# Two LRU tiles in flight with 64-row gate products, pooling spread over filler and merge, 512-wide v and half of q/k, and another order of the filler

## The chip, the cores and the metric

One core of one Trainium2 chip runs the whole kernel in one launch. The metric is the device time of that launch in microseconds (us). Engines are named as the profile names them: PE (matmuls), PEld (the loading of a matmul's stationary operand), DVE, ACT, POOL, and SP, which issues most DMAs.

## The reference, cut to what matters

One encoder layer on 1024 tokens of width 1024. The input is normalised and multiplied by a 1024 x 9216 matrix; the columns are then split into branches of 512 columns and four merge gates of 1024:

```
z = rms_norm(x) @ w_in
a_x, a_g, q, k, v, b_g, c_x, c_g, d_x, d_g, merge = split(z)
y_a = rglru(a_x) * silu(a_g)                  # gated linear recurrence, both directions
y_b = neighbourhood_attention(q, k, v) * silu(b_g)
y_c = s5(c_x) * silu(c_g)                     # state space mixer, then a GLU
y_d = pool(d_x) * silu(d_g)                   # windowed means of 2, 4, 8, 16, then a 128x128 product
merged = sum_n (y_n @ w_branch[n]) * sigmoid(merge_n)
x = x + merged @ w_out
x = x + sigmoid(x @ ple_gate) * (p @ ple_proj)
```

In the recurrence (`rglru`) the convolved input `xc` passes two gates for each direction, `sigmoid(xb @ w + b)`, with eight 64 x 64 blocks in each weight, and then a scan `h[t] = a[t] h[t-1] + b[t]`.

## The kernel before, in words

Every large product is made in three passes to keep fp32 accuracy: each operand is split into a rounded part H (an ACT copy to fp32r) and a rest L (a DVE subtraction), and `mm3` (L87 to L94) issues H by H, H by L and L by H into the same PSUM bank. So a product over 1024 rows of contraction is 8 x 3 = 24 matmuls.

`z_gen` (L156) makes the product with `w_in` in units: one unit is 128 columns by 512 tokens, 24 matmuls 512 wide, into a PSUM bank of tag `z` (or alternately `z` and `t` when `zt` is "zt"). It is a Python generator, and its units are the filler, `fill`: most of the kernel's PE work is in it, 104 units, and they need nothing but the normalised input and their weights. A list in `run` (L1283) gives their order: the s5 input, the silu gates of branches (`branch_gate`, with a sigmoid on ACT and a product on DVE) and the merge gates (`gates`, a sigmoid on ACT alone).

The stages stand in this order: `start` (norm, the product p @ ple_proj, the first q/k), `attention`, `s5`, `glu`, `lru`, the rest of the filler, `pool` together with the loading of the first merge operand (`y_split`), `merge` (four branches in the order 1, 0, 2, 3) and `final`. In attention the loop itself takes filler: one step of the generator `side` after each of the 8 units of a round. The rounds 0 and 1 take the q/k product of round 2 and 3 (`at_z`, 8 steps of 24 matmuls, 256 wide); rounds 2 and 3 take one unit of `fill` each time. In `s5`, `glu` and `lru` a planner, `drive` (L187), adds up the PE and DVE microseconds that the stage and the filler declare in their `yield`, the stage's DVE figure multiplied by SC = (1.25, 1.35, 0.95), and emits filler as long as PE is behind. The order in which instructions are emitted is a priority only: the order in each engine's queue is fixed before the run by a list scheduler that works on modelled times, so that an instruction whose operands and buffers are there can come ahead of one that was emitted earlier.

`q`, `k` and `v` are made per token tile: `tok_gen` (L208) takes 128 tokens as the stationary operand and 256 columns of weights as the moving one. There are six such products of 8 tiles: four of q/k (one for each round, 128 columns of q and 128 of k) and two of v. `attention` runs v's two, then q/k of round 1, then the rounds.

An attention unit (`at_units`, L511) makes scores for two heads (4 matmuls into tag `s`), adds the bias and takes the maximum on DVE, exponentiates on ACT, normalises on DVE, transposes by 6 PE transposes into tag `t`, and copies them out on ACT; after every second unit `at_values` issues 24 matmuls of 128 x 64 with the values.

`lru` (L610) works on four tiles of 128 channels. A tile (`lru_tile`, L633) convolves on DVE, splits `xc`, and multiplies by four 128 x 128 gate matrices that hold two 64 x 64 blocks on the diagonal and zeros elsewhere (written by a POOL memset): 4 matrices x 2 halves x 3 passes = 24 matmuls, with a sigmoid on ACT after each half. The tanh, exp and square root on ACT, seven passes and two scans on DVE follow. All of its buffers are single, except for the input `up`.

`pool` (L695) generates its own 8 units of z and, at every second one, runs a `pool_tile` (L719): window sums by doubling adds on DVE, a split, 6 matmuls into tag `o`. `merge` (L1174) multiplies the branches; each result of 12 matmuls goes to `s` or `o` and is gated and summed on DVE.

## Time and profile before

| what | value |
|---|---|
| time, median of 3 runs (lowest to highest) | 1385.28 us (1384.99 to 1386.05) |
| the profiled execution's own time | 1385.52 us |
| its span, first to last instruction | 1383.7 us |
| matmuls in the span | 7450 |
| DMA | 181.99 MB, mean 132 GB/s |

A "start" in the views is counted from the first instruction of the span. A matmul's duration there is from its start to its modelled end, and a following one starts before that; the spacing of starts, not the duration, says how much of PE one takes. A granted clock of 1.00 is the higher of the two levels, 2.4 GHz.

### The profile page before, as it was taken

How to read it: one execution, taken by the hardware profiler on the slowest of the kernel's cores; microseconds unless marked ns; L12 is line 12 of the kernel's file. 1: busy time of each engine (PE TensorE's matmuls, PEld its weight loads, DVE VectorE, ACT ScalarE, POOL GpSimd, SP SyncE). 2: the span in 40 equal slices, each digit the busy share in tenths (PEclk: the TensorE clock that was granted, in tenths of full speed). 3: DMA queues.
4: the chain of work that ended last, by engine and by line, in shares of the span. 5: the costliest groups of instructions: out<-in, count | busy, mean ns of one | idle time of the engine just before them, and what ended most of it. 6: DMA issues, size and time to landing. Idle time of an engine off the chain costs nothing.

```text
span 1383.7 us, 19208 instructions
## 1 busy us (share of the span) xinstructions
PE 1368.5 (99%) x7450; PEld 1159.6 (84%) x7450; DVE 843.8 (61%) x1592; ACT 521.3 (38%) x825; POOL 20.6 (1%) x81
## 2 busy tenths in 40 slices
PE   7999999999999999999999999999999999999998
PEld 6999998888788888788888888888888888888886
DVE  6551766455299797979757556636566767732332
ACT  6542676588332222222243662644312212211211
POOL 2200000000000000000000000000000000000000
PEclk9999999999999999999999999999999999999999
DMA  9451223433443142324264143135527655333543
GB/s 323 130 146 59 72 77 118 133 105 109 100 127 99 61 129 89 114 88 127 91 213 142 35 140 110 61 137 188 213 94 258 206 175 176 135 108 128 179 144 119
DMA packets 141054, 181.99 MB, mean 132 GB/s; under 512 B 29200, under 2 KB 100888, under 8 KB 140962
## 3 DMA queue, kind: packets, MB, share of 16 engines
q1 hardware_dynamic: 140610, 180.72, 40.4%
q8 instruction: 59, 0.97, 0.3%
q14 instruction: 33, 0.27, 0.1%
q0 software_dynamic: 352, 0.03, 0.0%
HBM read 127.05 MB, written 54.03 MB: 131 GB/s over the span
## 4 chain that ended last, share of the span: by engine, by line
PE 93%; DVE 5%; DMA 1%; ACT 1%; issue 0%; SPq 0%; DVEq 0%
PE ps_z L92 19%; PE ps_z L93 19%; PE ps_z L94 19%; PE ps_t L97 4%; PE ps_t L93 4%; PE ps_t L92 4%; PE ps_t L94 4%; PE ps_o L92 3%; PE ps_o L93 3%; PE ps_o L94 3%; PE ps_s L92 3%; PE ps_s L93 3%; PE ps_s L94 3%; PE ps_o L578 2%; PE ps_s L543 2%; PE ps_s L1068 1%
## 5 line engine op out<-in xcount | busy, mean ns | idle before, releaser
L92 PE MATMUL ps_z<-hnH,wh 128*128 128x512 f32 x744 | 293.2, 394 | 2.0 <-DVE bgt L58 2.0
L93 PE MATMUL ps_z<-hnL,wh 128*128 128x512 f32 x744 | 292.0, 392 | 0.0
L94 PE MATMUL ps_z<-hnH,wl 128*128 128x512 f32 x744 | 291.9, 392 | 0.0
L64 DVE TENSOR_TENSOR wl<-wr,wh 128x1024 fp32r<-128x1024 f32 x88 | 107.4, 1221 | 110.4 <-ACT wh L80 109.6
L92 PEld LDWEIGHTS ps_z<-hnH,wh 128*128 128x128 f32 x744 | 139.8, 188 | 30.8 <-DVE bgt L58 2.4
L94 PEld LDWEIGHTS ps_z<-hnH,wl 128*128 128x128 f32 x744 | 139.8, 188 | 28.5 <-issue 0.4
L93 PEld LDWEIGHTS ps_z<-hnL,wh 128*128 128x128 f32 x744 | 139.8, 188 | 27.9 <-issue 0.4
L80 ACT ACTIVATE wh<-wr 128x1024 fp32r<-128x1024 f32 x88 | 93.0, 1059 | 166.3 <-PE ps_z L93 81.2
L92 PE MATMUL ps_z<-wh,hnH 128*128 128x256 f32 x384 | 108.3, 285 | 0.5 <-ACT zqk L80 0.5
L94 PE MATMUL ps_z<-wh,hnL 128*128 128x256 f32 x384 | 108.5, 287 | 0.0
L93 PE MATMUL ps_z<-wl,hnH 128*128 128x256 f32 x384 | 108.1, 283 | 0.0
L93 PE MATMUL ps_t<-hnL,wh 128*128 128x512 f32 x216 | 84.2, 390 | 0.0
L92 PE MATMUL ps_t<-hnH,wh 128*128 128x512 f32 x216 | 84.1, 389 | 0.0
L94 PE MATMUL ps_t<-hnH,wl 128*128 128x512 f32 x216 | 84.0, 389 | 0.0
L92 PEld LDWEIGHTS ps_z<-wh,hnH 128*128 128x128 f32 x384 | 73.2, 192 | 1.2 <-ACT zqk L80 1.2
L93 PEld LDWEIGHTS ps_z<-wl,hnH 128*128 128x128 f32 x384 | 73.5, 191 | 0.0
L94 PEld LDWEIGHTS ps_z<-wh,hnL 128*128 128x128 f32 x384 | 72.9, 192 | 0.0
L94 PE MATMUL ps_z<-wh,mL 128*128 128x512 f32 x128 | 51.0, 399 | 0.0
L549 DVE CUSTOM_DVE_ANT_0 sc<-ps_s,bias 128x384 f32<-128x384 f32 x64 | 34.2, 554 | 27.2 <-PE ps_s L543 14.6
L92 PE MATMUL ps_o<-myH,wh 128*128 128x512 f32 x128 | 49.9, 390 | 0.4 <-DVE pm L67 0.4
L92 PE MATMUL ps_z<-wh,mH 128*128 128x512 f32 x128 | 50.2, 393 | 0.0
L93 PE MATMUL ps_z<-wl,mH 128*128 128x512 f32 x128 | 50.0, 391 | 0.0
(371 smaller groups left out, 2596.9 us busy)
## 6 DMA issues: line engine op xcount, KB each, us to landing
wr<-in_w_in_dram SPq DMA_DIRECT2D x32, 1024.0 KB, 5.3
gd<-gz SPq DMA_DIRECT2D x32, 512.0 KB, 2.9
mgt<-gd SPq DMA_DIRECT2D x32, 512.0 KB, 4.2
sg<-bgt SPq DMA_DIRECT2D x16, 512.0 KB, 3.1
my<-yd SPq DMA_DIRECT2D x16, 512.0 KB, 4.2
mbr<-in_w_branch_dram SPq DMA_DIRECT2D x8, 1024.0 KB, 6.7
bias<-E SPq DMA_DIRECT2D x128, 48.0 KB, 2.0
xt<-in_x_dram SPq DMA_DIRECT2D x8, 512.0 KB, 10.0
```

Source lines behind the costliest of these rows:

```text
L64: self.nc.vector.tensor_tensor(out, a, b, ALU.subtract)
L80: return self.nc.scalar.activation(out, a, AF.Copy)
L92: mm(ps, aH, bH, start=(k == 0), stop=False)
L93: mm(ps, aH, bL, start=False, stop=False)
L94: mm(ps, aL, bH, start=False, stop=(k == n - 1))
L97: self.nc.tensor.transpose(ps, src, self.ident[:k, :k])
L543: nc.tensor.matmul(pss[h], q[h][:, qs], km[h][(slice(0, 128),) + ks], start=(p == 0), stop=(p == 1))
L549: nc.vector.tensor_tensor_reduce(sc, pss[h], bias[g][h][:, VIDX[j], :], 1.0, -3e38, ALU.add, ALU.max, mx)
L578: m = self.nc.tensor.matmul(po[64 * h:64 * h + 64, j * 128:j * 128 + 128], vb[:, g + c, j, h * 64:h * 64 + 64], PT[h][:, c * 128:c * 128 + ...
L1068: nc.tensor.matmul(py[:, c], Q[k][:, a, 1:9, :].rearrange("p t c -> p (t c)"), X[k][:, c], start=False, stop=(k == 1))
```

## The change

- v is made in one product 512 wide (8 tiles of 24 matmuls) instead of two 256 wide. The q/k products of rounds 2 and 3 are made as one product 512 wide too (`at_pair`), those of rounds 0 and 1 stay. Both take their split weights from three of the usual buffers (`whl`) and from the two buffers `gz`. The staging tile of v is 512 wide, and there is one of them instead of two.
- In attention, the q/k product of round 1 is no longer ahead of the rounds: two of its tiles stand beside each of the first four units of round 0. The pair's 8 tiles stand beside units 6 and 7 of round 0 and 0 to 5 of round 1. Units 6 and 7 of round 1 take one unit of filler each, and in rounds 2 and 3 every second unit does.
- SC becomes (1.5, 1.35, 0.8). The filler has another order, and the pooling input's 8 units are in it, ahead of the last merge gate. Three units (before: two) stand between s5 and glu, and their first matmul is placed behind the last s5 matmul on PE.
- In `lru_tile` the buffers of `xc`, the four gate outputs and `ls` are doubled. The gate weights are stored without zeros: 64 rows for each block, both directions beside each other. A gate product is 6 matmuls of 64 rows and 128 columns, 512 wide, alternating between rows 64 to 127 and rows 0 to 63 in a fixed order and into two banks (`s` and `o`). ACT then evacuates each of the four 64 x 512 quarters with its own bias; the biases come by two more small DMAs and two more PE transposes in `consts`.
- `pool` is cut in steps of its own and works from inputs that filler has already made. Its steps stand beside the rest of the filler (after the five steps of the first `y_split`) and then beside the merge's products. It uses `z` and `t` banks, and `whl` buffers for its weights.

```diff
-SC = (1.25, 1.35, 0.95)
+SC = (1.5, 1.35, 0.8)
...
+                if self.hold is not None:
+                    self.behind(first, self.hold)
                 yield 5.2, 0.55 + (f(ct, hf, ps) or 0.0)
...
+            br = tmp.tile([8, 2, 2, 64], F32, name="br")
+            for k, n in enumerate(("lru_b_r", "lru_b_i")):
+                nc.gpsimd.dma_start(br[:, k], i[n].rearrange("d (g c) -> g d c", c=64))
+                self.tr(pt[:, 80 + 8 * k:88 + 8 * k], br[:, k].rearrange("g d c -> g (d c)"), 8)
...
+        raw_v = self.wide_load("w_in", 2048)
...
-            self.tok_product(self.hnH, self.hnL, raw, put_v)
...
+        for t, ps in self.qkv_tiles(raw_v):
+            v = ap.tile([128, 512], F32, tag="vtok", name="vtok")
+            self.copy_a(v, ps)
+            nc.sync.dma_start(vd[t * 128:t * 128 + 128, :], v)
...
             for u, _ in enumerate(self.at_units(ap, rd, qk, bias, vd)):
-                next(side, None)
-                if u == 3:
+                if rd == 0 and u < 4:
+                    next(side)
+                    next(side)
+                elif rd < 2 or u % 2:
+                    next(side, None)
+                step = (rd, u)
+                if step == (0, 2):
+                    raw1 = self.qk_load(1)
+                if step in ((0, 3), (1, 5)):
+                    prep = self.at_prep(ap, rd + 1, zq[rd + 1])
+                    nxt = next(prep)
+                if step in ((0, 3), (0, 4), (1, 5), (1, 6), (2, 3)):
                     next(prep, None)
...
+                if step == (0, 5):
+                    side = self.at_pair(raw1)
+                    zq += next(side)
+                if step == (1, 5):
+                    side = fill
...
+    def qkv_tiles(self, raws):
+
+        hl = []
+        for q in range(4):
+            if q < 3:
+                H, L = self.whl([128, 2, 512])
+            else:
+                H, L = (self.gzp.tile([128, 2, 512], F32R, tag="gz", name="w" + c) for c in "hl")
+            self.split(H, L, raws[q // 2][:, q % 2 * 2:q % 2 * 2 + 2, :])
+            hl += [(H[:, k, :], L[:, k, :]) for k in range(2)]
+        for t in range(8):
+            ps = self.ps("z")
+            c = slice(t * 128, t * 128 + 128)
+            self.mm3(ps, [(self.hnH[k][:, c], self.hnL[k][:, c]) + hl[k] for k in range(8)])
+            yield t, ps
...
+        for m in range(2):
             for hf in range(2):
...
+                self.lru_gates(ct, m, slice(hf * 512, hf * 512 + 512), gH, gL, xH, xL, sg)
+                yield 0.9, 3.5
...
+        for k, (g, x) in enumerate(((gH, xH), (gH, xL), (gL, xH))):
+            for b in (1, 0):
+                r = rows[b]
+                i = self.nc.tensor.matmul(pss[b], g[r, m, :], x[r, c], start=(k == 0), stop=(k == 2))
+                if last is not None:
+                    self.behind(i, last)
+                last = i
+        for b, r in enumerate(rows):
+            for d, q in enumerate(rows):
+                self.act(sg[2 * m + d][r, c], pss[b][q], AF.Sigmoid,
+                         bias=self.gb[q, m, 2 * ct + b:2 * ct + b + 1])
...
+    def behind(self, later, earlier):
+
+        self.tc.add_manual_dep(later.ins, earlier.ins.name, mybir.DependencyInfo(
+            mybir.DependencyClass.NoSync, mybir.DependencyReason.DATA), reason="one run")
...
+            fill = self.z_gen([self.s5_u(), self.branch_gate(2, 3584), self.gates(1), self.gates(3),
+                               self.branch_gate(0, 512), self.gates(2), self.branch_gate(3, 4608),
+                               self.branch_gate(1, 2560), self.pool_part(), self.gates(0)])
...
-            next(fill)
-            next(fill)
             self.zt = "zt"
+            self.hold = self.last_y
+            for _ in range(3):
+                next(fill)
+            self.hold = None
             self.drive(self.glu(), fill, SC[1])
...
+                self.drive(self.lru(), fill, SC[2])
...
+                    side = itertools.chain(self.y_split(mp, mp, 1, Y), pool)
+                    for _ in fill:
                         next(side, None)
+                    while len(Y) < 4:
+                        next(side)
+                    self.merge(mp, mq, (1, 0, 2, 3), Y, side)
```

## Rows read from the trace of the kernel before

**Rows 1.** The page's part 1: busy time, share of the span, instructions.

```profile
PE 1368.5 (99%) x7450; PEld 1159.6 (84%) x7450; DVE 843.8 (61%) x1592; ACT 521.3 (38%) x825; POOL 20.6 (1%) x81
```

**Rows 2.** The page's part 4: the chain that ended last, by engine.

```profile
PE 93%; DVE 5%; DMA 1%; ACT 1%; issue 0%; SPq 0%; DVEq 0%
```

**Rows 3.** Windows by stage: length, then PE, PEld, DVE, ACT, POOL busy, clock, DMA.

```profile
262.00:366.00 104.00, 104.00 (x658) 87.02 (x656) 51.17 (x171) 78.05 (x139) 0.73 (x2) 1.00 0.35 107
407.00:703.00 296.00, 293.99 (x1702) 246.22 (x1701) 248.73 (x465) 65.56 (x104) 0.00 (x0) 1.00 0.33 102
750.00:952.00 202.00, 202.00 (x891) 166.94 (x890) 113.53 (x97) 103.14 (x125) 1.84 (x7) 1.00 0.29 101
1018.00:1200.00 182.00, 181.61 (x801) 150.01 (x800) 127.26 (x162) 41.47 (x41) 0.00 (x0) 1.00 0.53 178
```

**Rows 4.** Timeline of PE, q/k products 256 wide: start, duration, instruction.

```profile
152.52 0.28 PE L92 MATMUL ps_z<-wh,hnH 128*128 128x256 f32 x1
...
153.96 0.28 PE L92 MATMUL ps_z<-wh,hnH 128*128 128x256 f32 x1
```

**Rows 5.** Timeline of PE, filler units 512 wide.

```profile
860.14 0.39 PE L92 MATMUL ps_z<-hnH,wh 128*128 128x512 f32 x1
...
863.09 0.39 PE L93 MATMUL ps_z<-hnL,wh 128*128 128x512 f32 x1
```

**Rows 6.** Timeline of PE, LRU gate products between filler matmuls.

```profile
769.24 0.39 PE L93 MATMUL ps_s<-xL,gH 128*128 128x512 f32 x1
...
771.09 0.40 PE L93 MATMUL ps_z<-hnL,wh 128*128 128x512 f32 x1
```

**Rows 7.** Timeline of PE, s5's small-array products between filler (windows 426:432, 430.93:431.2).

```profile
429.47 0.39 PE L93 MATMUL ps_z<-hnL,wh 128*128 128x512 f32 x1
429.79 1.42 PE L973 MATMUL ps_s<-Q,Bb 64*32 64x128 f32 x60
...
430.69 0.52 PE L973 MATMUL ps_s<-Q,Bb 64*32 64x128 f32 x12
431.14 0.50 PE L94 MATMUL ps_z<-hnH,wl 128*128 128x512 f32 x1
431.48 0.39 PE L92 MATMUL ps_z<-hnH,wh 128*128 128x512 f32 x1
```

**Rows 8.** Groups of ACT by line and shape: count, busy us, mean ns, idle before.

```profile
L76 ACT ACTIVATE sg<-ps_o,vt 128x512 f32<-128x512 f32 x16 | 11.1, 695 | 0.0
L81 ACT ACTIVATE qd<-ps_t,gain 64x512 fp32r<-64x512 f32 x32 | 21.8, 683 | 7.3 <-PE ps_t L97 5.5 <-DVE ql L67 1.1
```

**Rows 9.** Timeline of PE in s5: a wait and what ended it.

```profile
556.35 0.50 PE L92 MATMUL ps_z<-hnH,wh 128*128 128x512 f32 x1 [1.65 <-DVE bgt L58]
```

**Rows 10.** Groups of PE from 158 to 366.7 us, the four rounds.

```profile
L92 PE MATMUL ps_z<-hnH,wh 128*128 128x512 f32 x157 | 61.9, 394 | 0.0
...
L92 PE MATMUL ps_z<-wh,hnH 128*128 128x256 f32 x80 | 22.8, 287 | 0.2 <-ACT zqk L80 0.2
```

**Rows 11.** The tiles yb and wh: durations min/median/max, first and last start.

```profile
L570 SPq DMA_DIRECT2D yd<-yb x4: 319/370/382, 200.4 to 366.7; - x4
L92 PE MATMUL ps_z<-hnH,wh x12: 387/390/397, 207.2 to 215.8; 128*128 128x512 f32 x12
```

**Rows 12.** Timeline of PE in round 0: the value products of successive unit pairs.

```profile
168.49 1.53 PE L578 MATMUL ps_o<-PT,vb 128*64 128x128 f32 x24
...
175.96 1.53 PE L578 MATMUL ps_o<-PT,vb 128*64 128x128 f32 x24
```

**Rows 13.** From the LRU to the merge: tile up, timeline of DVE, tile myL, timeline of PE.

```profile
L80 ACT ACTIVATE up<-ps_z x4: 598/598/599, 749.7 to 863.7; 128x512 f32<-128x512 f32 x4
...
950.84 1.22 DVE L58 TENSOR_TENSOR ls<-ls,sgl 128x1024 f32<-128x1024 f32 x1
...
L64 DVE TENSOR_TENSOR myL<-my,myH x4: 1225/1225/1226, 963.8 to 979.9; 128x1024 fp32r<-128x1024 f32 x4
...
1018.92 0.39 PE L92 MATMUL ps_s<-myH,wh 128*128 128x512 f32 x1
```

More of the change, by code (lines that the diff above doesn't have):

```diff
@@ L91, in mm3 @@
         for k, (aH, aL, bH, bL) in enumerate(pairs):
-            mm(ps, aH, bH, start=(k == 0), stop=False)
+            i = mm(ps, aH, bH, start=(k == 0), stop=False)
+            first = i if k == 0 else first
             mm(ps, aH, bL, start=False, stop=False)
             mm(ps, aL, bH, start=False, stop=(k == n - 1))
+        return first
     def tr(self, ps, src, k):
@@ L178, in z_gen @@
                 t = slice(hf * 512, hf * 512 + 512)
-                self.mm3(ps, [(H[:, k, :], L[:, k, :], self.hnH[k][:, t], self.hnL[k][:, t])
-                              for k in range(8)])
+                first = self.mm3(ps, [(H[:, k, :], L[:, k, :], self.hnH[k][:, t], self.hnL[k][:, t])
+                                      for k in range(8)])
+                if self.hold is not None:
+                    self.behind(first, self.hold)
                 yield 5.2, 0.55 + (f(ct, hf, ps) or 0.0)
@@ L216, in tok_gen @@
             yield 2.6, 0.0
-    def tok_product(self, aH, aL, raw, consume):
-        for _ in self.tok_gen(aH, aL, raw, consume):
-            pass
     def consts(self):
@@ L400, in attention @@
         vd = self.dp.tile([S, W], F32, name="vd")
-        z = [self.at_z(rd) if rd else self.z0 for rd in range(4)]
         zq = [self.zq0]
@@ L572, in at_values @@
     def at_values(self, po, vb, g, held, last):
-        before = last.ins
+        before = last
         for j, PT in held:
@@ L581, in at_values @@
                     if before is not None:
-                        self.tc.add_manual_dep(m.ins, before.name, mybir.DependencyInfo(
-                            mybir.DependencyClass.NoSync, mybir.DependencyReason.DATA), reason="one run")
+                        self.behind(m, before)
                     before = None
@@ L692, in lru_tile, with lru_gates, pool_u, pool_part @@
         nc.sync.dma_start(self.yd[0][ct * 128:ct * 128 + 128, :], s[0])
+    def lru_gates(self, ct, m, c, gH, gL, xH, xL, sg):
+        rows = [slice(64 * b, 64 * b + 64) for b in range(2)]
+        pss = [self.ps("so"[b]) for b in range(2)]
+        last = None
+        for k, (g, x) in enumerate(((gH, xH), (gH, xL), (gL, xH))):
[12 more added lines that the diff above has]
+            mybir.DependencyClass.NoSync, mybir.DependencyReason.DATA), reason="one run")
+    def pool_u(self, pu):
+        self.up = [pu.tile([128, 1040], F32, name=f"pup{k}") for k in range(4)]
+        for u in self.up:
+            self.nc.gpsimd.memset(u[:, 0:8], 0.0)
+            self.nc.gpsimd.memset(u[:, 1032:1040], 0.0)
+    def pool_part(self):
+        def put(ct, hf, ps):
+            self.copy_a(self.up[ct][:, 8 + hf * 512:8 + hf * 512 + 512], ps)
+        return 4096, 2, put
     def pool(self, pp):
-        nc, i = self.nc, self.i
+        nc = self.nc
         ef = pp.tile([128, 4, 16], F32, name="ef")
@@ L702, in pool @@
                 nc.gpsimd.memset(ef[:, g, 8 + t:9 + t], w / (w - t))
-        us = {}
-        def put_u(ct, hf, ps):
-            if hf == 0:
-                u = pp.tile([128, 1040], F32, tag="up", name="pup", bufs=2)
-                nc.gpsimd.memset(u[:, 0:8], 0.0)
-                nc.gpsimd.memset(u[:, 1032:1040], 0.0)
-                us[ct] = u
-            self.copy_a(us[ct][:, 8 + hf * 512:8 + hf * 512 + 512], ps)
-            if hf == 1:
-                self.pool_tile(pp, ct, us[ct], ef)
-            return 4.0
-        for c in self.z_gen([(4096, 2, put_u)]):
-            yield c
+        for g in range(4):
+            yield from self.pool_tile(pp, g, self.up[g], ef)
     def pool_tile(self, pp, g, u, ef):
@@ L1172, in branch_products, with merge @@
                     yield m, hf, gt, pb
-    def merge(self, mp, mq, order, Y):
+    def merge(self, mp, mq, order, Y, side):
         acc = [self.big.tile([128, 1024], F32, tag=f"bH{k}", name="acc") for k in range(8)]
@@ L1196, in merge @@
                     next(pre, None)
+                next(side, None)
             Y = nxt
@@ L1234, in final @@
             self.fw = itertools.count()
-            blocks = [(n, nb) for n in ("w_out", "ple_gate") for nb in range(2)]
+            blocks = [(n, 512 * nb) for n in ("w_out", "ple_gate") for nb in range(2)]
             raws = [self.wide_load(*blocks[0])]
-            for m, (n, nb) in enumerate(blocks):
+            for m in range(4):
+                nb = m % 2
                 if m < 2:
```

140 lines of the change are left out of this document (70 added, 70 removed).

## The prediction

> **What bounds the kernel now.** I read the page's busy line first: PE is busy for 1368.5 of 1383.7 us, DVE for 61% and ACT for 38% [rows 1]. A busy PE need not be at its peak, so the chain of waits comes next: PE holds 93% of the chain that ended last, DVE 5% [rows 2]. The windows by stage say the same from the rounds of attention to the end of the merge: PE is idle for 2.0 us in all of s5 and for 0.4 us in the merge, at a granted clock of 1.00, that is 2.4 GHz; DVE is nearest to a bound in s5, with 249 of 296 us [rows 3]. So there is next to no waiting to win back. The kernel gets faster only by what PE is spared, and slower by any new wait of PE. The spared time must be counted by the spacing of starts, since a matmul's duration covers the next start.
>
> **The change part by part.** The sum is made against the profiled execution, 1385.5 us, which is 0.2 us above the median of the runs; 1.8 us of it lie outside the span.
>
> *512-wide v and half of q/k.* Between 152.52 and 153.96 us lie 12 starts of 256-wide matmuls, 0.120 us each [rows 4]; between 860.14 and 863.09 lie 13 starts of 512-wide ones, 0.227 us each [rows 5]. Streaming 256 and 512 columns at 2.4 GHz takes 0.107 and 0.213 us, so each matmul pays about 0.013 us whatever its width, and 384 of 7450 matmuls go. Two old tiles take 48 x 0.120 = 5.76 us, a new one 24 x 0.227 = 5.45; v has 8 new tiles and the pair has 8: 16 x 0.31 = 5.0 us less. More cannot come of it, as no column is spared. Less can: a new tile wants all four splits of its weights, where the old one had two, so each of the two products could start a split late. The subtraction of such a split is 1.2 us by the same shape in rows 13; twice that leaves 2.6. I take 5.0: the last matmuls of the product before run meanwhile, and the fourth buffer pair (`gz`) is idle at that time. One staging tile for v instead of two is enough when a copy and its store end within a tile's 5.45 us; if SP is held by the value loads behind it, the second `z` bank covers one more tile.
>
> *Gate products of 64 rows.* The old ones: from 769.24 to 771.09 us lie eight starts, 0.231 us each [rows 6]; 96 of them are 22.2 us. The new ones are 96 too, in 16 runs of six, three for each half of the array's rows. If a half's matmul streams beside the other half's, a run is 3 x 0.227 = 0.68 us. What it costs to leave the full array and come back is read from s5's products of 64 rows and 32 columns. The step from a full matmul to the first small one is 0.32 us (429.47 to 429.79) instead of 0.227: +0.09. From 429.79 to 430.69, 48 small ones start 0.019 us apart; the last 12 need 0.23 at that rate, but the next full one starts 0.45 us after 430.69: +0.22. The full one after it is 0.34 us away: +0.11 [rows 7]. So a run costs 0.42 us beside its work. That makes 16 x (0.68 + 0.42) = 17.6 us, 4.6 us less than before. The bounds: if the switch were free, 10.9 us (11.3 less); if the halves did not stream side by side, 16 x (6 x 0.231 + 0.42) = 28.9 us (6.7 more). I take the value between, because the small products show both the switch and the overlap: a 128-column stream is 0.053 us at 2.4 GHz, and they start 0.019 apart [rows 7].
>
> The Trainium skill has a rule that speaks against this edit: changing the tiling mode drains the engine, while tiles of one mode work independently ("TensorEngine Tiling (Array Packing)", section Key Properties). Rows 7 agree with both halves of it; the page gives no price, and by the rule without one the term would lie anywhere from 11.3 less upward.
>
> The evacuation grows. A 64 x 512 activation takes as long as a 128 x 512 one, 0.683 against 0.695 us [rows 8], since ACT pays for columns. Before there were 32 such sigmoids, now 64: +22 us on ACT in the LRU, which had 103 of 202 us there [rows 3]. Each run then needs 4 x 0.69 = 2.8 us of ACT. It costs PE nothing while filler is there to run; without that cover it goes into the length of the LRU (second rival).
>
> *More filler in s5, less in attention and LRU.* The filler is moved, not removed, so PE's sum stays; what can change is waiting. Adding up the declared figures, `drive` gave s5 about 47 units and gives it 57 now. In the old list 24 of the 47 were silu units, whose product on DVE delays the release of their bank; such a product ended the wait of 1.65 us at 556 us [rows 9]. By the new list 14 of 57 are, and DVE's share falls. Of s5's 2.0 us of waits I take 1.0 as gone (bounds 0 and 2.0).
>
> *Attention with less filler.* Its loop now asks for filler in every second unit of rounds 2 and 3 and for none in units 4 and 5 of round 0. I cost this at 0, because the loop's place is only a priority. In the old rounds 157 first-pass matmuls of filler ran, 157 / 8 = 19.6 units where the loop asked for 16 [rows 10]. They began at 207.2 us, when only the first of four rounds had been stored (200.4), though the loop hands out filler from round 2 on [rows 11]. The scheduler pulls work ahead where PE would idle. The price without that cover is the third rival. ACT, 78 of 104 us in the later rounds [rows 3], gets relief, as fewer sigmoids stand between its exponentials.
>
> *Pooling beside filler and merge, three held units, consts.* The pool's 8 units of z and 24 matmuls stay. Its DVE work moves into a merge that has DVE at 127 of 182 us [rows 3], with the lightest part, the first branch, first: 0. The three held units give 16.4 us of PE work behind the last s5 product instead of 10.9 without the placing: 0. Two more small DMAs on POOL and two more transposes come well before PE reaches them: 0 (at most 0.2, two starts). The gate weights lose their POOL memset and keep their four DMAs a tile on SP.
>
> Sum: 1385.5 - 5.0 - 4.6 - 1.0 = 1374.9, so 1375 us. The term bounds by themselves give 1385.5 - 5.0 - 11.3 - 2.0 = 1367 and 1385.5 - 2.6 + 6.7 = 1389.6.
>
> **The rivals.**
>
> *The halves do not stream side by side.* For it: the only row products in the trace have 32 columns and four column groups, so their 0.019 us doesn't prove that two full-width halves overlap. Against it: 0.019 us is under half a stream. The gates then cost 6.7 us more, and the sum is 1385.5 - 5.0 + 6.7 - 1.0 = 1386.2: no change.
>
> *The LRU ends late, and PE runs dry ahead of the merge (the slower side).* The merge's first operand takes memory that the LRU holds. Before, the LRU lasted from 749.7 to 952.1 us, and the last split of that operand ended at 981.1, 29 us later; filler went on to 1018.9 [rows 13]. By the planner's figures 101 of the 112 units are handed out by the LRU's end, so LRU and tail together have 24 + 8 + 11 = 43 units, or 234 us with 5.45 us each, and 18 us of gates. If the scheduler runs 6 units ahead, as rows 10 suggest with its 3.6 in attention alone, 219 us are left. The LRU must then be done in 190. If it keeps its old 202 us, PE idles 12; if the 22 us of ACT lengthen it too, 34. I price it in the middle: 1375 + 23 = 1398. Against it: neither ACT (103) nor DVE (114) filled the 202 us [rows 3], so the single buffers and the amount of filler set that length, and two tiles in flight shorten it. The Trainium skill warns of the same place: tiling speeds up TensorE but not the evacuation of PSUM, which may become the bottleneck (same page, section PSUM Bottleneck); rows 8 agree with the cost for ACT.
>
> *Attention starves.* Of the 208.7 us of the old rounds filler took 3 x 157 x 0.23 and the 256-wide products 3 x 80 x 0.12, 137 us together [rows 10]; the 32 units' own matmuls are the rest, 2.2 us each. The fastest pace of units is two in 168.49 to 175.96, 3.74 us each [rows 12]. If the ten units without filler run at that pace with nothing beside them, PE idles 10 x 1.5 = 15 us: 1390. It decides as soon as the scheduler pulls nothing ahead; rows 11 are against it.
>
> *The switch is free.* Then 1367, as in the sum by bounds; rows 7 are against it.
>
> **How the numbers follow.** The forecast has 0.66, with a range of its own from 1369 to 1381; halves in sequence 0.10; late LRU 0.09; starving attention 0.09; free switch 0.06. The likeliest gives 1375. From 1366 to 1391 it takes in the free switch, the sequence and about all of the starving case, and leaves out most of the late LRU and the tails: a little over 8 in 10. What a measurement of this kernel tells from no change is about 0.2%, 2.8 us. Faster by more than that: the forecast, the free switch and a little of the slow cases made good elsewhere, 0.73. Within it: the sequence and small new waits, 0.12. Slower: 0.15.
>
> **What would show it.** The 256-wide matmuls fall to a third of their number, and 512-wide ones start 0.227 us apart in v. A gate run's six starts come in pairs, a few hundredths of a us between the two halves, about 0.23 us from pair to pair, and the first filler matmul starts late by some 0.2 us; if the six are 0.23 us apart each, the first rival holds. In s5 PE's idle time falls below 2 us. PE's idle time in the windows of attention and between the LRU's last product and the merge stays under 1 us; 10 us and more there would make the prediction wrong, with the LRU's last product or the scores as what ended the wait. The sigmoids of the gates are 64 of 64 x 512 at 0.69 us.

## The result, and the profile after

The changed kernel took 1408.95 us (median of 4 runs, 1407.08 to 1409.89) against 1385.13 us for the kernel before on the same chip: a ratio of 1.0169, 95% interval 1.0152 to 1.0187. Forecast were 1375 us, in a range from 1366 to 1391. In the profiled execution the span grew by 23.9 us, from 1383.7 to 1407.6.

The page of the changed kernel: TensorE's busy line, the granted clock in 40 slices, the chain that ended last.

```profile
PE 1376.7 (98%) x7068; PEld 1138.6 (81%) x7068; DVE 843.0 (60%) x1593; ACT 547.5 (39%) x851; POOL 19.9 (1%) x79
...
PEclk9999899999999999999999999999999999999999
...
PE 92%; ACT 4%; DVE 3%; DMA 1%; issue 1%; SPq 0%; ACTq 0%
```

PE has 382 matmuls fewer than in [rows 1], as it should, and yet is busy for 8.2 us more. The chain still belongs to PE, but ACT has 4% of it where [rows 2] had 1%. For a kernel whose PE is always busy I split PE's time by what it computes: for all matmuls of a kind, the time from start to next start, added up. So a wait counts with the kind that ran just before it, and a slow clock with the kinds that ran through it.

| us (matmuls) | before | after | c1_gates | f4_both |
|---|---|---|---|---|
| norm | 10.5 | 14.9 | 10.5 | 10.3 |
| input products, 256 wide | 141.5 (1152) | 50.1 (384) | 141.0 (1152) | 94.5 (768) |
| input products, 512 wide | 664.2 (2880) | 763.4 (3264) | 677.1 (2880) | 707.0 (3072) |
| attention | 73.8 | 79.0 | 73.7 | 73.9 |
| s5 | 48.8 | 55.3 | 48.8 | 46.4 |
| recurrence's gates (96) | 22.1 | 17.5 | 14.4 | 22.1 |
| merge (768) | 174.3 | 178.9 | 174.3 | 175.9 |
| all | 1376.1 | 1399.9 | 1382.1 | 1372.2 |

(The last two columns are experiments, below. The other kinds, 241 to 242 us in each column, are left out.) The gates fell by 4.6 us, and some 3 of their 17.5 us are waits among and behind the pairs: c1's pairs, which do not wait, take 14.4. All else that should fall or stay rose, the input products of both widths together from 805.7 to 813.5. The stretches where it happened, in windows of the changed kernel (length; PE, PEld, DVE, ACT, POOL busy; clock; DMA):

```profile
46.00:66.00 20.00, 17.53 (x123) 17.10 (x123) 8.36 (x13) 9.52 (x18) 0.73 (x2) 0.83 0.30 95
164.00:182.00 18.00, 13.30 (x44) 9.98 (x43) 9.43 (x21) 12.06 (x24) 0.00 (x0) 0.62 0.00 1
697.00:711.00 14.00, 8.17 (x34) 7.18 (x33) 6.96 (x11) 2.14 (x3) 0.00 (x0) 0.63 0.13 43
826.00:854.00 28.00, 24.82 (x110) 17.67 (x109) 16.47 (x17) 27.32 (x34) 0.00 (x0) 1.00 0.06 20
```

The kernel before has no such stretch in its norm, in round 0 or in its recurrence:

```profile
46.00:60.00 14.00, 14.00 (x122) 13.85 (x120) 7.02 (x15) 6.20 (x12) 1.98 (x4) 1.00 0.43 135
160.00:185.00 25.00, 24.53 (x218) 23.27 (x217) 19.84 (x70) 18.96 (x46) 0.00 (x0) 1.00 0.26 75
840.00:880.00 40.00, 40.00 (x178) 33.06 (x177) 15.79 (x14) 16.78 (x21) 0.00 (x0) 1.00 0.31 105
```

In the changed kernel's four PE idles 2.5, 4.7, 5.8 and 3.2 us, and in the first three the clock is low as well. At its two levels, a mean of 0.83 over 20 us is 6.8 us at 1.2 GHz, 0.62 over 18 is 13.7, and 0.63 over 14 is 10.4. The Trainium skill's table of the clock's states has these two levels, 1.2 GHz for an idle TensorE and 2.4 GHz for a busy one ("TensorE: Matmul & The Clock Gate", Part 1). The starts of 512-wide matmuls agree, 0.43 us apart in these stretches (175.35 to 175.78 below) and 0.227 elsewhere.

*46 to 66 us, the norm.* Timeline of ACT, then of PE; a bracket tells the idle time ahead of an instruction and what ended it:

```profile
46.67 1.06 ACT L82 ACTIVATE wh<-wr 128x1024 fp32r<-128x1024 f32 x1 [3.91 <-DMA wr<-in_w_in_dram]
47.63 1.25 ACT L83 ACTIVATE hnH<-ps_t,gT 128x512 fp32r<-128x512 f32 x2
```

```profile
48.35 0.58 PE L94 MATMUL ps_z<-wh,hnH 128*128 128x256 f32 x1 [3.77 <-ACT hnH L83]
48.73 0.41 PE L96 MATMUL ps_z<-wl,hnH 128*128 128x256 f32 x1
```

A split of v's wide weights stands in ACT's queue ahead of the norm's copies `hnH`, and waits for its DMA. Behind it wait the copies, and PE for them.

*164 to 182 us, round 0.* PE waits for the preparation of round 1 (`km`), for the copy `PT` that frees the transposes' bank, and then for `zqk`:

```profile
167.28 1.08 PE L101 MATMUL ps_t<-ident,zqk 128*128 128x128 f32 x4 [2.17 <-DVE km L69]
...
169.57 0.90 PE L101 MATMUL ps_t<-ident,sc 128*128 128x128 f32 x3 [0.58 <-ACT PT L82]
...
174.76 0.79 PE L94 MATMUL ps_z<-wh,hnH 128*128 128x512 f32 x1 [1.95 <-ACT zqk L82]
175.35 0.63 PE L96 MATMUL ps_z<-wl,hnH 128*128 128x512 f32 x1
175.78 0.63 PE L97 MATMUL ps_z<-wh,hnL 128*128 128x512 f32 x1
```

*697 to 711 us, the end of s5.* The three units are held behind the last s5 product, so in front of it PE has none:

```profile
701.76 0.80 PE L1139 MATMUL ps_s<-Xr,Q 128*128 128x128 f32 x2 [4.17 <-DVE Xr L66]
704.23 0.79 PE L1139 MATMUL ps_s<-Xi,Q 128*128 128x128 f32 x2 [1.67 <-DVE Xi L63]
```

*826 to 854 us, the recurrence.* ACT's queue there, and PE behind it:

```profile
842.45 1.38 ACT L78 ACTIVATE sg<-ps_o,gb 64x512 f32<-64x512 f32 x2
843.85 1.40 ACT L78 ACTIVATE sg<-ps_s,gb 64x512 f32<-64x512 f32 x2
845.27 1.06 ACT L82 ACTIVATE xH<-xc 128x1024 fp32r<-128x1024 f32 x1
846.24 1.04 ACT L82 ACTIVATE wh<-wr 128x1024 fp32r<-128x1024 f32 x1
```

```profile
846.38 0.49 PE L750 MATMUL ps_o<-xH,gH 64*128 64x512 f32 x1 [1.12 <-ACT xH L82]
847.33 0.50 PE L94 MATMUL ps_z<-hnH,wh 128*128 128x512 f32 x1 [0.46 <-ACT wh L82]
```

The gate pairs themselves, which answer to [rows 6, 7], do what the forecast said:

```profile
821.59 0.40 PE L97 MATMUL ps_z<-hnH,wl 128*128 128x512 f32 x1
821.92 0.50 PE L750 MATMUL ps_o<-xL,gH 64*128 64x512 f32 x1
821.92 0.50 PE L750 MATMUL ps_s<-xL,gH 64*128 64x512 f32 x1
822.26 0.39 PE L750 MATMUL ps_s<-xH,gL 64*128 64x512 f32 x1
822.26 0.39 PE L750 MATMUL ps_o<-xH,gL 64*128 64x512 f32 x1
822.48 0.39 PE L750 MATMUL ps_s<-xL,gH 64*128 64x512 f32 x1
```

Two halves start together. The step in takes 0.33 us, the first pair is followed by the second after 0.34, and later pairs are 0.22 apart.

### The profile page after: what moved, and what is told of

Same layout as the page of the kernel before. It is cut to its first block, busy times and chain, and to the rows that moved or that the text cites. A ratio compares the mean times of both kernels' runs of the same rounds, so it can differ in the third digit from the quotient of the medians.

```text
span 1407.6 us, 18440 instructions
## 1 busy us (share of the span) xinstructions
PE 1376.7 (98%) x7068; PEld 1138.6 (81%) x7068; DVE 843.0 (60%) x1593; ACT 547.5 (39%) x851; POOL 19.9 (1%) x79
## 4 chain that ended last, share of the span: by engine, by line
PE 92%; ACT 4%; DVE 3%; DMA 1%; issue 1%; SPq 0%; ACTq 0%
PE ps_z L94 19%; PE ps_z L97 19%; PE ps_z L96 19%; PE ps_t L101 4%; PE ps_t L94 3%; PE ps_t L96 3%; PE ps_t L97 3%; PE ps_s L97 2%; PE ps_o L97 2%; PE ps_s L94 2%; PE ps_o L96 2%; PE ps_s L96 2%; PE ps_o L94 2%; PE ps_o L632 2%; PE ps_s L597 1%; PE ps_s L1139 1%
## 5 line engine op out<-in xcount | busy, mean ns | idle before, releaser
L97 PE MATMUL ps_z<-hnH,wl 128*128 128x512 f32 x752 | 295.9, 393 | 1.1 <-DVE wl L66 1.1
L96 PEld LDWEIGHTS ps_z<-hnL,wh 128*128 128x128 f32 x752 | 141.5, 188 | 29.3 <-issue 1.3
L94 PE MATMUL ps_z<-wh,hnH 128*128 128x256 f32 (+1 forms) x256 | 88.6, 349 | 5.9 <-ACT hnH L83 3.8
L96 PE MATMUL ps_z<-wl,hnH 128*128 128x256 f32 (+1 forms) x256 | 88.4, 346 | 0.0
L97 PE MATMUL ps_z<-wh,hnL 128*128 128x256 f32 (+1 forms) x256 | 87.6, 347 | 0.1
L78 ACT ACTIVATE gz<-ps_z 128x512 f32<-128x512 f32 x54 | 31.9, 590 | 77.2 <-PE ps_z L97 41.8
L94 PEld LDWEIGHTS ps_z<-wh,hnH 128*128 128x128 f32 x256 | 50.1, 196 | 11.6 <-ACT hnH L83 4.0
L96 PEld LDWEIGHTS ps_z<-wl,hnH 128*128 128x128 f32 x256 | 50.1, 196 | 4.7
L97 PEld LDWEIGHTS ps_z<-wh,hnL 128*128 128x128 f32 x256 | 49.4, 195 | 5.4 <-DVE hnL L69 0.4
L97 PE MATMUL ps_s<-myH,wl 128*128 128x512 f32 x128 | 50.6, 395 | 0.2 <-DVE wl L66 0.2
L96 PE MATMUL ps_o<-myL,wh 128*128 128x512 f32 x128 | 50.5, 395 | 0.0
```

Of the source, the lines that this page charges most:

```text
L78: self.nc.scalar.activation(out, a, f, **kw)
L94: i = mm(ps, aH, bH, start=(k == 0), stop=False)
L96: mm(ps, aH, bL, start=False, stop=False)
L97: mm(ps, aL, bH, start=False, stop=(k == n - 1))
```

## The experiments

My theory after the traces (Theory A below): these are four separate losses, each set by what stands in one queue, and the merge's slower products (178.9 for 174.3 us) are a fifth. The rival (Theory B): the time goes in the long stages, and what is won early is given back.

### Three losses taken out of the changed kernel

**a1_nohold**

```diff
-            self.hold = self.last_y
             for _ in range(3):
                 next(fill)
-            self.hold = None
```

> The changed kernel, but the three units of filler behind s5 are not placed behind the last s5 product. Theory A (the loss is a handful of starts that TensorE waits for, each followed by a stretch at half clock): TensorE's two waits before the last s5 products (4.2 us on Xr, 1.7 us on Xi) and the half-clock stretch from 699.8 to 710 go, some 9 us: about 1400 us. Theory B (the time is lost in the long stages, the recurrence and the merge, and what is won earlier is given back there as a wait): 1407 to 1410 us, with the idle time coming back in front of the gated unit, where the held units had been TensorE's only work.

Measured: 1402.70 us, ratio to before 1.0121 (1.0103 to 1.0139). The waits between 690 and 720 us are gone, and 6.3 of 23.8 us come back, less than the 9 expected. In the profiled execution the clock fell at another place instead: between 836 and 848 us it is 0.72, behind waits of 1.1, 0.5 and 0.5 us in the recurrence like those that left it at 1.00 in the changed kernel. Its four executions go from 1398.5 to 1404.7 us.

**a2_norm**

```diff
-        for t, ps in self.qkv_tiles(raw_v):
+        for t, ps in self.qkv_tiles(raw_v, self.last_n):
...
-            self.split(H, L, raws[q // 2][:, q % 2 * 2:q % 2 * 2 + 2, :])
+            self.split(H, L, raws[q // 2][:, q % 2 * 2:q % 2 * 2 + 2, :], after)
```

(`last_n` is ACT's last copy of the norm.)

> The changed kernel, but ScalarE's copies of v's raw weights stand behind its last copy of the normalised input. Theory A: the 3.8 us wait on hnH at 48 us and the half-clock stretch behind it go, some 7 us: about 1402 us, with the last hnL copy back near 59 us. Theory B: v's weights are then late for its first tile, so that the wait moves to v's first product and the time stays within 2 us of 1409.

Measured: 1402.57 us, 1.0122 (1.0107 to 1.0137): 6.4 us back. The last `hnL` ends at 60.1 us instead of 66.8.

**a3_att**, and **a4_three**, which is a1, a2 and a3 together

```diff
         side = self.at_z(1)
         zq.append(next(side))
...
+        for _ in side:
+            pass
...
+            if rd == 0:
+                next(prep, None)
+                side = self.at_pair(raw1)
+                zq += next(side)
```

In both, the preparation of round 1 writes queries over those that round 0's first half still reads, so later units of round 0 compute with other queries than the reference's; the amount of work is the same.

> The changed kernel with the attention's work in another order: the q/k product of round 1 wholly ahead of the rounds, the whole preparation of round 1 at the start of round 0, the 512-wide product for rounds 2 and 3 beside all eight units of round 0, filler at every second unit of rounds 1 to 3. Theory A: the five waits of TensorE between 167 and 175 us (about 9 us together) and the half clock until 181 us go, the preparation of round 1 costs about 2 us of its own; some 8 to 10 us less: about 1400 us. Theory B: rounds 1 to 3 starve with filler in every second unit only, and the half clock appears there; within 3 us of 1409 or above.

> All three of the edits together. Theory A: the savings add, 9 + 7 + 9 us, because each stretch lies on TensorE's path and is given back nowhere: about 1384 us, the time of the kernel before. Theory B (given back later): less than half of the sum, above 1396 us.

Measured: a3 1414.53 us (1.0211), a4 1397.32 us (1.0082; 1.0065 to 1.0099). Theory A misses on a3, which is 5.6 us slower than the changed kernel, as Theory B had it, and on a4, which lies above B's 1396. a4 shows a reason: PE still waits 2.7 us on `km`, and between 120 and 160 us it is idle for 3.8 us. By the code the 512-wide product writes both `zqk` buffers, so it must follow round 1's preparation in any order, and the traces show nothing beside the preparation on PE. a4 gives back 11.6 us in all; a1 and a2 by themselves give 12.6. So either the two add and the order wins nothing, or they add a little less; a1 with a2 alone was not run.

### Parts of the change, put into the kernel before

**c1_gates**: the 64-row gates (`lru_gates`, the bias table) as in the change. **c2_widev**: v in one 512-wide product, split behind the norm. **c3_both**.

```diff
-                self.mm3(ps, [(gH[:, m, :], gL[:, m, :], xH[:, c], xL[:, c])])
-                self.act(o[:, c], ps, AF.Sigmoid, bias=v[:, 5 + m:6 + m])
...
+                self.lru_gates(ct, m, slice(hf * 512, hf * 512 + 512), gH, gL, xH, xL, sg)
```

```diff
-            self.tok_product(self.hnH, self.hnL, raw, put_v)
...
+        for t, ps in self.qkv_tiles(raw_v, self.last_n):
```

> The kernel before with one part of the change: the recurrence's gates as pairs of 64-row products (and their bias table), its buffers, its order and all else as before. Theory A (the gates are worth what the prediction said, the loss lies elsewhere): gates 44.5 us of TensorE in the first kernel against 39.4 in the changed one, both with their waits; 4 to 5 us less than before, about 1381 us. Theory B (the 64 evacuations of half a tile hold ScalarE, which splits the next weights and recurrence tiles, and TensorE waits 4 to 5 us as it does at 846 to 852 us in the changed kernel): same as before within 1 us or slower.

> The kernel before with one part of the change: v as one 512-wide product, with its weights' splits behind the norm's last copy so that they hold nothing up. Theory A: 384 products of 256 columns at 0.123 us become 192 of 512 columns at 0.227 us, 47.2 against 43.6: 3 to 4 us less, about 1382 us. Theory B (the wide tiles wait for weights or for a buffer): no gain.

> The kernel before with both of these parts. Theory A: they add, 7 to 8 us less than before, about 1377.5 us: faster than both kernels. Theory B (one gives back what the other wins, in the slack ahead of the merge): 1381 us or above.

Measured: c1 1391.54 us, 1.0045 (1.0032 to 1.0058). c2 1384.33 us, 0.9991 (0.9983 to 1.0000). c3 1389.37 us, 1.0028 (1.0018 to 1.0039). Theory B holds for c1 and c3; c2's 1.1 us lie between its two theories, at the edge of what the runs tell apart. The pairs are a surprise. (The 44.5 and 39.4 us expected for gates include some 22 us of the GLU's own.) They take 7.7 us off the gates (table), more than in the changed kernel, and make the kernel 6.1 us slower. c1's PE, between the recurrence and the merge:

```profile
1001.04 1.22 PE L92 MATMUL ps_o<-pmH,pwH 128*128 128x512 f32 x2 [5.48 <-ACT pmH L80]
1002.05 0.63 PE L92 MATMUL ps_z<-hnH,wh 128*128 128x512 f32 x1
```

The recurrence's last gate product ends 9.7 us later (944.3 for 934.6), the pooling behind it comes late, and PE waits 5.5 us and goes on at 1.2 GHz. Two shorter waits, of 1.1 us for `wh` at 794 and of 1.7 us for `wl` at 855, come before. v wide wins 1.1 us; on PE 141.5 - 95.4 less and 708.4 - 664.2 more, 1.9 us.

**g1_evac64** tells whether it is the pairs or their evacuation:

```diff
-                self.act(o[:, c], ps, AF.Sigmoid, bias=v[:, 5 + m:6 + m])
+                for q in (slice(0, 64), slice(64, 128)):
+                    self.act(o[q, c], ps[q], AF.Sigmoid, bias=v[q, 5 + m:6 + m])
```

> The kernel before with nothing changed but the evacuations of the recurrence's gates: each 128-row sigmoid is cut into two of 64 rows, 64 in all; TensorE's products stay as they were. Theory A (what the pairs lose is ScalarE's time: 64 evacuations at 0.68 us instead of 32 at 0.69, 21.6 us more): TensorE's gates stay near 22.1 us, and yet the kernel is 8 to 14 us slower, the 6 us that the pairs lost in the kernel before plus the 8 that they won on TensorE: about 1397 us, with the wait in front of the pooling's products near 1000 us that the pairs had (5.5 us). Theory B (the loss comes from the pairs themselves, from their switches or their tables): within 1.5 us of before.

Measured: 1398.42 us, 1.0093 (1.0075 to 1.0111): 12.7 us slower with not one product changed (gates 22.1 us). Theory A, though the wait is in another place than forecast. g1's ACT, then PE:

```profile
791.98 1.28 ACT L76 ACT_TABLE_LOAD   x1
793.28 1.38 ACT L76 ACTIVATE sg<-ps_s,vt 64x512 f32<-64x512 f32 x2
794.68 0.63 ACT L80 ACTIVATE gH<-gw 128x512 fp32r<-128x512 f32 x1
795.34 1.38 ACT L76 ACTIVATE sg<-ps_o,vt 64x512 f32<-64x512 f32 x2
796.74 1.06 ACT L80 ACTIVATE wh<-wr 128x1024 fp32r<-128x1024 f32 x1
```

```profile
797.85 0.80 PE L92 MATMUL ps_z<-hnH,wh 128*128 128x512 f32 x1 [4.84 <-ACT wh L80]
798.44 0.63 PE L93 MATMUL ps_z<-hnL,wh 128*128 128x512 f32 x1
```

The filler's next weights `wh` stand behind the sigmoids; a second wait, of 3.1 us for `wl`, comes at 853. Halves of an evacuation cost 0.684 us each, as [rows 8] say; and between 700 and 1060 us ACT loads its tables 21 times instead of 14 (18 in c1), 1.28 us each. The prediction's second rival was right that the evacuations would tell. It was wrong on where PE would feel them: in the middle of the recurrence, with filler at hand, and not ahead of the merge. The Trainium skill says that tiling speeds up TensorE but not the evacuation of PSUM, and that the copy may become the bottleneck after a fourfold speedup ("TensorEngine Tiling (Array Packing)", section PSUM Bottleneck). Here the doubled evacuations cost 12.7 us with PE's products unchanged.

### The changed kernel repaired, and its gates and attention exchanged

**e3_place** is a1 and a2 together and

```diff
-                with tc.tile_pool(name="po", bufs=1, reuse_waits="tile") as pp, \
-                        tc.tile_pool(name="mp", bufs=1, reuse_waits="tile") as mp, \
-                        tc.tile_pool(name="mq", bufs=1, reuse_waits="tile") as mq:
+                with tc.tile_pool(name="mp", bufs=1, reuse_waits="tile") as mp, \
+                        tc.tile_pool(name="mq", bufs=1, reuse_waits="tile") as mq, \
+                        tc.tile_pool(name="po", bufs=1, reuse_waits="tile") as pp:
...
-        self.up = [pu.tile([128, 1040], F32, name=f"pup{k}") for k in range(4)]
+        self.up = [pu.tile([128, 1088], F32, name=f"pup{k}")[:, 0:1040] for k in range(4)]
```

> The changed kernel without the held units and with the norm's order mended, and then the merge's two pools put ahead of the pooling's in memory, so that the merge's operands lie lower (from 134208 bytes of a partition instead of 146624) and at the same offset in 2 KB as the rest. The first two edits alone should give 1396 us (6.3 and 6.4 us less, if they add). Theory A (where the operands lie sets the merge's pace of 0.232 us for each product instead of 0.227): the pace falls to 0.227, 768 x 0.005 = 4 us less: about 1392 us. Theory B (the pace comes from the pooling beside it, or from elsewhere): 0.232 stays, 1396 us.

Measured: 1390.54 us, 1.0034 (1.0022 to 1.0045); the merge's products are back at 0.227 us. If a1 and a2 add, that is 5.8 us for the place; the products alone are 3.7 us faster (178.9 to 175.2). e3's six executions go from 1387.3 to 1392.7 us, and the profiled one is near the lowest.

**f1_gates128**: e3 with the gates of the kernel before. **f2_att256**: e3 with its attention, v wide. **f4_both**. **f5_onedeep**: e3 without the `bufs=2` of `xc`, `sg`, `ls`.

```diff
-                self.lru_gates(ct, m, slice(hf * 512, hf * 512 + 512), gH, gL, xH, xL, sg)
...
+                self.mm3(ps, [(gH[:, m, :], gL[:, m, :], xH[:, c], xL[:, c])])
```

```diff
-                    side = self.at_pair(raw1)
...
+                side = z[rd + 2]
```

> The changed kernel with its three repairs (no held units, the norm's order, the merge's place; 1390.5 us), and in it the gates of the kernel before: 96 products on all rows instead of the pairs, 32 evacuations of 128 rows instead of 64 of 64 rows; recurrence two tiles deep as in the changed kernel. Theory A (the pairs win nothing once ScalarE's 22 us more of evacuation hold up the splits): TensorE's gates 22.1 instead of 17.0 us, but its waits on ScalarE's and VectorE's splits between 804 and 833 us (5 us) go: same within 1.5 us. Theory B (with the pooling beside the merge the evacuations are hidden and the pairs win their 5 to 8 us): 4 us or more slower, 1395 us or above.

> The same repaired kernel (1390.5 us) with the attention of the kernel before, but v 512 wide: the q/k products of rounds 1 to 3 in 256 columns, round 1's whole ahead of the rounds, those of rounds 2 and 3 beside rounds 0 and 1, filler at every unit of rounds 2 and 3. Theory A (round 0 loses some 9 us to waits and the half clock behind them, because the preparation of round 1 and the product for rounds 2 and 3 must follow one another within it): 384 more products of 256 columns cost 1.5 us, the 9 us go: about 1383 us. Theory B (filler that the attention takes is missed later, in s5 or the recurrence): 1388 us or above.

> Both: the repaired kernel with the gates and the attention of the kernel before. What is left of the change is v 512 wide, the recurrence two tiles deep, and the pooling beside filler and merge. Theory A: about 1382 us, the gates neutral, the attention's 7 us won; faster than both kernels by some 3 us. Theory B (the pairs win): 1387 us or above.

> The repaired kernel (1390.5 us) with the recurrence's buffers one tile deep as before, its gates in pairs. Theory A (two tiles deep keeps the tail of the recurrence off TensorE's path): it comes out 2 us or more slower, with waits of TensorE on the recurrence's splits above 5 us in all. Theory B (the depth buys nothing, since there is filler to run beside it): within 1.5 us.

Measured, before at 1386.14: f1 1391.51 us (1.0037), f2 1397.30 (1.0081; 1.0067 to 1.0094), f4 1381.38 (0.9966; 0.9954 to 0.9979), f5 1393.81 (1.0059). So f4, with the old gates and the old attention, beats both kernels. Theory A holds for f1, f4 and f5, Theory B for f2. Gates and attention cannot be priced apart. With old gates the old attention is worth 10.1 us (f1 to f4), and in f4 PE waits nowhere between 150 and 180 us; with the pairs the old attention costs 6.8 (e3 to f2). With the new attention the pairs are worth 1 us at most (f1 to e3), with the old one they cost 15.9 (f4 to f2). Two tiles deep is worth some 3 us (f5 to e3; the intervals touch), and PE's waits in the recurrence are 5.6 us without it, 3.2 with it. f2's PE from 1000 to 1060 us, where the merge begins:

```profile
PE ps_s L96 <- ACT myH L82: 4.8, 2, 3.2
PE ps_s L96 <- ACT wh L82: 2.4, 1, 2.4
PE ps_s L98 <- DVE myL L66: 2.1, 1, 2.1
PE ps_o L96 <- DVE acc L60: 1.7, 1, 1.7
```

(waited for: us, times, longest). The old attention uses more filler, less is left beside the recurrence, and the merge's first operand `myH`, late by the pairs' evacuations, comes bare. With the old gates (f4) the same attention has one wait there, of 1.3 us.

**g2_lessfill** (f2) and **g4_lessfill128** (f4) test that:

```diff
-                next(side, None)
+                if rd < 2 or u % 2:
+                    next(side, None)
```

> The repaired kernel with the old attention (1397.3 us), with filler at every second unit only in rounds 2 and 3, so that 8 units more (43 us of TensorE's work) are left for s5 and the recurrence. Theory A (the pairs lost 16 us there because the filler ran out beside the recurrence, and ScalarE's and VectorE's late work was left bare at the merge's start, 1010 to 1053 us): the waits at the merge's start go, the attention loses 2 to 4 us: about 1385 us. Theory B (the merge's late start has another cause): 1395 us or above.

> The kernel with the repairs, the old attention and the old gates (1381.4 us), with filler at every second unit only in rounds 2 and 3. Theory A (with whole-row gates ScalarE has the room, filler was not short, and the only wait of 1.5 us at the merge's start is all there is to win): the attention loses 2 to 4 us and the merge wins 1.5: 1382 to 1384 us. Theory B (filler is short here too): below 1380 us.

Measured: g2 1385.56 us, 1.0000 (0.9990 to 1.0009), 11.7 less than f2, with 1.4 us of waits left at the merge's start: theory A. g4 1389.39 us, 1.0028 (1.0018 to 1.0039), 8.0 more than f4: neither theory. Its ACT and PE:

```profile
811.32 1.28 ACT L78 ACT_TABLE_LOAD   x1
812.62 0.69 ACT L78 ACTIVATE sg<-ps_o,vt 128x512 f32<-128x512 f32 x1
813.20 0.68 ACT L78 ACTIVATE sg<-ps_s,vt 128x512 f32<-128x512 f32 x1
813.77 1.06 ACT L82 ACTIVATE wh<-wr 128x1024 fp32r<-128x1024 f32 x1
```

```profile
814.88 0.50 PE L96 MATMUL ps_z<-hnH,wh 128*128 128x512 f32 x1 [2.16 <-ACT wh L82]
...
817.41 0.79 PE L96 MATMUL ps_s<-xH,gH 128*128 128x512 f32 x1 [1.80 <-ACT xH L82]
```

With filler shifted by eight units, a weight split meets a run of table loads and sigmoids that it misses in f4. So the amount of filler is only a part of it; where it falls on ACT's queue is another. And with this filler the pairs win: g2 is 3.8 us faster than g4, where f2 is 15.9 slower than f4.

### What slows the merge's products

Three versions of f4 that differ in where the merge's operands lie in a partition (what is allocated next to them moves too). In f4 they begin at 134208 bytes, 64 past a multiple of 512; in the changed kernel at 146624, 192 past.

```diff
-pu.tile([128, 1088], F32, name=f"pup{k}")[:, 0:1040]
+pu.tile([128, 1040], F32, name=f"pup{k}")
```

for **g3_offset**, and for **h1_low192** the same with 1064 columns allocated; **h2_high64** is h1 with the pools in the changed kernel's order. Their operands begin at 133440 bytes (320 past a multiple of 512), 133824 (192 past) and 147008 (64 past).

> The kernel with the repairs, the old attention and the old gates (1381.4 us), with 192 bytes less in front of the merge's pools: its operands then begin at 320 bytes past a multiple of 512 instead of 64, and still lie low in memory. Theory A (the offset sets the pace of the merge's products: 64 bytes, as the weights', gives 0.227 us, 192 bytes gave 0.232): the pace is 0.232 or so again, 4 us slower. Theory B (what set the pace was how high the operands lay, or the pools' order): 0.227 stays.

> The kernel with the repairs, the old attention and the old gates (1381.4 us; 0.227 us for each product of the merge), with the padding chosen so that the merge's operands lie low as there (from 133824 bytes), but at 192 bytes past a multiple of 512, the offset that they had in the changed kernel. Theory A (the offset of 192 sets the slow pace): 0.232, about 4 us slower, 1385 us. Theory B (the height or the pools' order sets it): 0.227, 1381 us.

> The same kernel with the pools in the changed kernel's order, the pooling's ahead, so that the merge's operands lie high as there (from 147008 to 228900 bytes), but at 64 bytes past a multiple of 512. Theory A: 0.227, 1381 us. Theory B: 0.232 from the first product to the last, about 1385 us.

Measured: g3 1381.15 us (0.9974), h1 1385.97 (1.0005; 0.9995 to 1.0015), h2 1381.03 (0.9972; 0.9961 to 0.9983). Groups of PE from 1060 to 1180 us of the changed kernel, h1, h2 and the kernel before, one each (count, busy us, mean ns):

```profile
L94 PE MATMUL ps_s<-myH,wh 128*128 128x512 f32 x84 | 33.1, 395 | 0.0
```

```profile
L96 PE MATMUL ps_s<-myH,wh 128*128 128x512 f32 x84 | 33.2, 395 | 0.0
```

```profile
L96 PE MATMUL ps_s<-myH,wh 128*128 128x512 f32 x88 | 34.3, 389 | 0.0
```

```profile
L92 PE MATMUL ps_s<-myH,wh 128*128 128x512 f32 x88 | 34.2, 389 | 0.0
```

An offset of 192 is slow low in memory (h1) as it is high (the changed kernel); 64 is fast high (h2) as low (f4). Start to start that is 0.233 us in the mean in the first two and 0.227 in the last two; over the whole merge, 180.8 us in h1 and 175.8 in h2. The offset sets the pace, not the height. g3's 320 is fast, against what I expected of it. The stationary weights `wh` begin 64 bytes past a multiple of 512 in all of these but the kernel before, where all begin at 0; so whether the offset itself counts or its distance from theirs is not shown.

## Why the prediction was wrong

**The pieces.** PE's own work came out near the forecast; what failed are waits and a pace that the sum had at nothing. In the order in which I took them out: norm 6.4, held units 6.3, merge's place 5.8, round 0 10.1, less 1 that the pairs win beside the new attention, less the 4.8 by which f4, with what is left of the change, lies below the kernel before (1386.14 to 1381.38): 22.8 of the 23.8 us. This sum closes by its making, since each kernel is the one before it less a part; it is no proof that the parts are independent, and each is known to some 2 us. In another order gates and attention swap their prices: by way of f2 the new attention wins 6.8 and the pairs cost 15.9. The other order of the filler and the new SC were not run by themselves; they are in f4 too.

**The wide product (-5.0).** Pace and count were right: the 256-wide matmuls fell to a third. v's half was forecast at 2.5 and is worth 1.9 on PE, 1.1 in time; the pair's half was not run by itself. The failed step is its lower bound, "each of the two products could start a split late". I looked for what the split delays behind PE and not for what stands behind it on ACT: the norm's copies, 6.4 us.

**The gates (-4.6).** 22.1 to 17.5 us is just the forecast 4.6, but by luck: the halves stream side by side and the switch is cheaper than was read from s5 (some 0.3 us a run beside its work, not 0.42), so that the bare pairs take 14.4 us (c1), and 3 us of waits make up the rest. The rival of halves in sequence is out. The failed step is "It costs PE nothing while filler is there to run". Filler is no cover for ACT, because filler's own weights are split on ACT. With what they win on PE taken off, the pairs cost 6.1 us in c1 and 15.9 from f4 to f2, and win 1.0 from f1 to e3 and 3.8 from g4 to g2, by what else is in that queue; the evacuations alone cost 12.7 in g1.

**More filler in s5 (-1.0).** Right where nothing is held: s5's products go from 48.8 to 46.4 us in f4, and its waits of [rows 9]'s kind are gone. In the changed kernel they came to 55.3 by the held units.

**The held units (0).** Failed step: I counted the work placed behind the last s5 product, and not that it was taken from in front of it. The chain `Xr`, `Xi` on DVE was then bare.

**Attention with less filler (0).** Failed step: "the loop's place is only a priority". The scheduler can pull ahead what is free to run; in round 0 nothing was pulled: the pair's tiles are held up behind round 1's preparation (the wait on `zqk` at 174.76 us), and the first unit of filler runs at 227.8 us, behind the pair's last tile. What kept filler from running earlier is not shown. [Rows 11] showed pulling from 207.2 us on, in a kernel without the pair. With the old gates this is worth 10.1 us (f1 to f4). The starving rival had a price of 15 us, but put eight of its ten bare units in rounds 2 and 3, where the changed kernel waits 0.3 us.

**Pooling beside the merge (0).** No wait above 0.2 us came of it. Its pools moved the merge's operands to another offset: 4.6 us on the products (174.3 to 178.9), 5.8 in time if a1 and a2 add. No row of before could have shown this.

**The late LRU** did not decide in the changed kernel, but it is what f2 shows, with the operand that the rival named, once filler is short.

**The clock.** The whole sum was made at 1.00. In the changed kernel the waits of the norm, of round 0 and of s5's end went with 7, 14 and 10 us at 1.2 GHz, so a wait can cost more than its length: 6.4 us came back for the 3.8 us at the norm. But this price is no constant. For like waits in round 0 the clock between 155 and 182 us is 0.75 in the changed kernel, 0.87 in f1 and 0.94 in e3. In e3 it differs from execution to execution: two at a mean clock of 0.997 and 0.999 took 1387 us, four at 0.993 to 0.995 took 1390 to 1393.

## What to carry to other kernels

When PE is always busy, cost each edit by the in-order queue that its helpers stand in: which copy, split or evacuation comes ahead of which, and what PE waits for behind it. Work that covers PE covers nothing if its own inputs pass through the loaded engine. Before counting work placed behind a point, ask what it leaves bare in front of it; and price a wait of several us with the slow clock behind it, as a range. When two parts of a change load the same queue, run all four combinations: here each part looked good or bad by what the other did.

## What the runs showed of the hardware

Products of 512 columns in the merge start 0.233 us apart in the mean, not 0.227, when the streamed operand begins 192 bytes past a multiple of 512; 0, 64 and 320 bytes gave 0.227, and no other offset was tried there. Over the merge's 768 products that is 3.7 us (the changed kernel to e3) to 5.0 us (h1 to h2). With PE's wait of 3.77 us at 48 us, the clock was low for 6.8 us; with the three waits of round 0 for 13.7; with the waits of 4.17 and 1.67 us at 701 for 10.4 in the window. In the recurrence, waits up to 1.1 us left it at 1.00 in the changed kernel (window 826 to 854), and like waits took it to 0.72 in a1 (window 836 to 848). The two halves of a pair of 64-row products, 128 columns wide, start within 0.02 us of each other; a step from or to the full array takes 0.31 to 0.34 us, and so does that from the first pair to the second, where full products are 0.227 apart.
